# Row sums of |x - y| on one core: rows 5 and 6 in halves, the last row in five pieces instead of four

## The chip, the cores and the metric

One core of one Trainium2 chip. The time of a kernel is the device time in microseconds (us); "the time" of a set of runs is their median. Every run told of here is fast (granted clock 1.00, and none over 1.5% above the fastest of its kernel). Ratios are the mean time of one kernel's fast runs over that of the other's fast runs of the same rounds, so they are not quite the ratio of the medians quoted beside them.

## The reference

```python
batch, dim = 1024, 4096
x, y = two float32 arrays of (1024, 4096), normally distributed
np.sum(np.abs(x - y), axis=-1).astype(np.float32)      # 1024 sums
```

The inputs are 33.55 MB, the output 4 KB.

## The kernel before

Each of 128 partitions has eight rows, `K = 8`, of `C = 4096` columns. Rows 0 to 3 (`xa`, `yb`) come first; rows 4 to 7 of x go to `xb`, and rows 4 to 7 of y go into the places of `yb` that the first four subtractions free (`H = 4`). VectorE subtracts, ScalarE takes the absolute value and sums along the row as it goes. The last row, row 7, comes in pieces, so that little is left to do after the last byte.

```python
PIECES = [1984, 1088, 640, 384]
ROW6 = [2048, 1024, 1024]
# ... (helpers that place the instructions, tensors, semaphores: cut)
    put(lambda: nc.sync.dma_start(out=xb[:, 0:H - 1, :], in_=xr[:, H:K - 1, :]).then_inc(s_xb, 16))
    for k in range(H - 1):                      # y of rows 4, 5, 6
        put(lambda: nc.sync.wait_ge(s_sub, k + 1))
        put(lambda: nc.sync.dma_start(out=yb[:, k, :], in_=yr[:, H + k, :]).then_inc(s_row[k], 16))
    o = 0
    for i, w in enumerate(PIECES):              # row 7, x and y of each piece
        c = slice(o, o + w)
        put(lambda: nc.sync.dma_start(out=xb[:, H - 1, c], in_=xr[:, K - 1, c]).then_inc(s_piece[i], 16))
        if i == 0:
            put(lambda: nc.sync.wait_ge(s_sub, H))
        put(lambda: nc.sync.dma_start(out=yb[:, H - 1, c], in_=yr[:, K - 1, c]).then_inc(s_piece[i], 16))
        o += w
# ... sub() is a subtraction on VectorE, absum() the ScalarE instruction after it
    for k in range(H - 2):                      # rows 4 and 5 whole
        sub(xb[:, k, :], yb[:, k, :], ([(s_xb, 16)] if k == 0 else []) + [(s_row[k], 16)])
        absum(xb[:, k, :], ro[:, H + k:H + k + 1], s_act)
    o = 0
    for i, w in enumerate(ROW6):                # row 6 in three
        c = slice(o, o + w)
        sub(xb[:, H - 2, c], yb[:, H - 2, c], [(s_row[H - 2], 16)] if i == 0 else [])
        absum(xb[:, H - 2, c], part6[:, i:i + 1], s_act)
        o += w
    # ... row 7: each piece but the last is subtracted and summed like this, into last[:, i];
    # the last is only subtracted, into last[:, n_part:], and a reduction then takes
    # the absolute value of the whole of `last` and sums it:
            put(lambda: nc.vector.wait_ge(s_end, n_part + 2))
            put(lambda: nc.vector.reduce_sum(out=ro[:, K - 1:K], in_=last, axis=AX, apply_absolute_value=True).then_inc(s_end, 1))
```

Of the kernel before, what the change touches and what calls it, by code (L numbers as in the profile page):

```python
# [5 lines left out]

F32 = mybir.dt.float32
ABS = mybir.ActivationFunctionType.Abs
AX = mybir.AxisListType.X

F32 = mybir.dt.float32
ABS = mybir.ActivationFunctionType.Abs
AX = mybir.AxisListType.X

PIECES = [1984, 1088, 640, 384]
ROW6 = [2048, 1024, 1024]


class Entry:


    def __init__(self, nc):
        self.nc = nc

    def put(self, emit, before="UnconditionalBranch"):
        nc = self.nc
        hook = nc.inst_callbacks[-1]
        lower = nc._always_lower_symbolic_ap
        nc.remove_inst_callback(hook)
        nc._always_lower_symbolic_ap = False  # L30
        here = nc.cur_bb.bb.instructions
        n = len(here)
        try:
            emit()
        finally:
            nc._always_lower_symbolic_ap = lower
            nc.push_inst_callback(hook)
        here = nc.cur_bb.bb.instructions
        main = nc.main_func.blocks[0].instructions
        while len(here) > n:  # L40
            mine = here.pop(n)
            first = next(i for i, x in enumerate(main) if x.engine == mine.engine and x.opcode == before)
            main.insert(first, mine)

    def at_end(self, emit):

        nc = self.nc
        hook = nc.inst_callbacks[-1]
        here = nc.cur_bb.bb.name
        done = []  # L50

        def closing(ins):
            if done or nc.cur_bb.bb.name == here or ins.engine != mybir.EngineType.SP:
                return
            done.append(ins)
            emit()

        nc.remove_inst_callback(hook)
        nc.push_inst_callback(closing)
        nc.push_inst_callback(hook)  # L60


@with_exitstack
def kernel(ctx, tc, x, y, axis, out):
    nc = tc.nc
    P = nc.NUM_PARTITIONS
    R, C = x.shape
    K = R // P
    xr = x.rearrange("(p k) c -> p k c", p=P, k=K)
    yr = y.rearrange("(p k) c -> p k c", p=P, k=K)  # L70
    orr = out.rearrange("(p k) -> p k", p=P, k=K)
    assert sum(PIECES) == C and sum(ROW6) == C
    n_part = len(PIECES) - 1
    n6 = len(ROW6)
    H = K // 2
    entry = Entry(nc)
    put = entry.put

    def sbuf(name, shape):
        return nc.alloc_sbuf_tensor(name, shape, F32).ap()  # L80

    xa = sbuf("xa_rows", [P, H, C])
    xb = sbuf("xb_rows", [P, H, C])

    yb = sbuf("yb_rows", [P, H, C])
    ro = sbuf("ro_sums", [P, K])
    part6 = sbuf("part6_sums", [P, n6])

    last = sbuf("last_piece", [P, n_part + PIECES[-1]])

    s_first = tc.alloc_semaphore("s_first")
    s_xb = tc.alloc_semaphore("s_xb")
    s_row = [tc.alloc_semaphore(f"s_row{k}") for k in range(H - 1)]
    s_piece = [tc.alloc_semaphore(f"s_piece{i}") for i in range(len(PIECES))]
    s_sub = tc.alloc_semaphore("s_sub")
    s_act = tc.alloc_semaphore("s_act")
    s_end = tc.alloc_semaphore("s_end")
    s_out = tc.alloc_semaphore("s_out")


    put(lambda: nc.sync.dma_start(out=xa, in_=xr[:, 0:H, :]).then_inc(s_first, 16), before="RegisterMove")
    put(lambda: nc.scalar.dma_start(out=yb, in_=yr[:, 0:H, :]).then_inc(s_first, 16), before="RegisterMove")
    put(lambda: nc.sync.dma_start(out=xb[:, 0:H - 1, :], in_=xr[:, H:K - 1, :]).then_inc(s_xb, 16))
    for k in range(H - 1):
# [3 lines that stand above are left out]
    for i, w in enumerate(PIECES):  # L108
# [8 lines that stand above are left out]
    count = [0, 0]  # L117

    def sub(tx, ty, waits):
        for s, v in waits:  # L120
            put(lambda: nc.vector.wait_ge(s, v))
        put(lambda: nc.vector.tensor_sub(out=tx, in0=tx, in1=ty).then_inc(s_sub, 1))  # L122
        count[0] += 1

    def absum(tx, to, sem):
        put(lambda: nc.scalar.wait_ge(s_sub, count[0]))
        put(lambda: nc.scalar.activation(tx, tx, ABS, accum_out=to).then_inc(sem, 1))  # L127
        count[1] += sem is s_act

    for k in range(H):  # L130
        sub(xa[:, k, :], yb[:, k, :], [(s_first, 32)] if k == 0 else [])
        absum(xa[:, k, :], ro[:, k:k + 1], s_act)
    for k in range(H - 2):
        sub(xb[:, k, :], yb[:, k, :], ([(s_xb, 16)] if k == 0 else []) + [(s_row[k], 16)])
        absum(xb[:, k, :], ro[:, H + k:H + k + 1], s_act)
    o = 0
    for i, w in enumerate(ROW6):
        c = slice(o, o + w)
        sub(xb[:, H - 2, c], yb[:, H - 2, c], [(s_row[H - 2], 16)] if i == 0 else [])
        absum(xb[:, H - 2, c], part6[:, i:i + 1], s_act)  # L140
        o += w
    done6 = count[1]
    o = 0
    for i, w in enumerate(PIECES):
        c = slice(o, o + w)
        tx, ty = xb[:, H - 1, c], yb[:, H - 1, c]
        if i == 1:
            put(lambda: nc.vector.wait_ge(s_act, done6))
            put(lambda: nc.vector.reduce_sum(out=ro[:, K - 2:K - 1], in_=part6, axis=AX).then_inc(s_end, 1))  # L149
        if i < n_part:  # L150
            sub(tx, ty, [(s_piece[i], 32)])
            absum(tx, last[:, i:i + 1], s_end)
        else:
            put(lambda: nc.vector.wait_ge(s_piece[i], 32))
            put(lambda: nc.vector.tensor_sub(out=last[:, n_part:n_part + w], in0=tx, in1=ty).then_inc(s_end, 1))  # L155
# [4 lines that stand above are left out]
    put(lambda: nc.sync.wait_ge(s_end, n_part + 3))  # L160
    put(lambda: nc.sync.dma_start(out=orr, in_=ro).then_inc(s_out, 16))
    entry.at_end(lambda: nc.sync.wait_ge(s_out, 16))


# [1 line left out]
_INS = ['x', 'y', 'axis']  # L166
_OUTS = [((1024,), 'float32')]

_NUMBERS = {'axis': -1}


# [26 lines left out]
```

## Time and profile before

| | before |
|---|---|
| time, median of 6 runs | 85.92 us (85.87 to 85.97); three of them, 85.94, were known when the prediction was made |
| span of the profiled run | 84.1 us |
| VectorE busy, ScalarE busy | 36.5 us (43%), 31.2 us (37%) |
| read from memory over the span | 33.55 MB, 399 GB/s |
| row 6's y landed, last piece landed | 70.40, 80.59 us |
| last subtraction ended, ScalarE ended, closing reduction | 81.17, 81.33, 81.36 to 81.92 us |

A landing is read off the timeline: where an instruction is marked as released by a load ("<-DMA"), it starts 0.02 us after the landing. In all lines shown, DVE is VectorE, ACT is ScalarE, SPq and ACTq are the instruction queues of SyncE and ScalarE, and L122 is line 122 of the kernel. Neither compute engine is busy half of the span, and the loads run until 80 us. So only the order of events after the loads' end can be shortened, and the loads' end itself. The lines are in the prediction.

### The profile page before, as it was taken

To read this page: it belongs to the slowest core of one execution; us is meant where nothing else is said; L and a number is where in the kernel's file an instruction comes from. 1 tells how busy PE (TensorE), PEld (TensorE's weight loads), DVE (VectorE), ACT (ScalarE), POOL (GpSimd) and SP (SyncE) were. 2 spreads that over 40 slices of the span, in tenths; PEclk is the share of its full clock that TensorE was granted. 3 is DMA by queue.
4 is the path that set the end of the run, shared out by engine and by line. 5 is a ranking of instruction groups with operands and counts; after the bars stand their busy time and mean duration, and the time that the engine had idled before them with its cause. 6 is when DMAs were issued, how large, how long until landed. Compare 5 with 4: busy or idle time off the path is not lost.

```text
span 84.1 us, 97 instructions
## 1 busy us (share of the span) xinstructions
DVE 36.5 (43%) x15; ACT 31.2 (37%) x25; POOL 0.2 (0%) x4
## 2 busy tenths in 40 slices
DVE  0000000000000000000399999999199897988770
ACT  5000000000000000000002979797970977999960
POOL 0000000000000000000000000000000000000000
DMA  9289999992999999479899888899999999999900
GB/s 499 125 374 499 499 499 499 499 436 125 436 499 499 499 499 499 187 343 467 374 491 631 374 374 374 374 397 460 405 444 421 421 448 385 419 411 406 366 4 2
DMA packets 2160, 33.56 MB, mean 399 GB/s; under 512 B 368, under 2 KB 624, under 8 KB 1392
## 3 DMA queue, kind: packets, MB, share of 16 engines
q1 hardware_dynamic: 2016, 25.17, 71.2%
q10 hardware_dynamic: 144, 8.39, 23.0%
HBM read 33.55 MB, written 0.00 MB: 399 GB/s over the span
## 4 chain that ended last, share of the span: by engine, by line
DMA 67%; DVE 16%; ACT 13%; ACTq 1%; issue 0%
DMA yb_rows<-in_y_dram 67%; ACT xb_rows L127 13%; DVE xa_rows L122 10%; DVE xb_rows L122 5%; ACTq L193 1%; DVE ro_sums L157 1%
## 5 line engine op out<-in xcount | busy, mean ns | idle before, releaser
L122 DVE TENSOR_TENSOR xa_rows<-xa_rows,yb_rows 128x4096 f32<-128x4096 f32 x4 | 17.4, 4420 | 41.4 <-DMA yb_rows<-in_y_dram 41.4
L127 ACT ACTIVATE xa_rows<-xa_rows 128x4096 f32<-128x4096 f32 x4 | 14.5, 3617 | 45.5 <-DVE xa_rows L122 45.5
L122 DVE TENSOR_TENSOR xb_rows<-xb_rows,yb_rows 128x4096 f32<-128x4096 f32 (+5 forms) x8 | 17.8, 2240 | 3.5 <-DMA yb_rows<-in_y_dram 3.4
L127 ACT ACTIVATE xb_rows<-xb_rows 128x4096 f32<-128x4096 f32 (+5 forms) x8 | 14.9, 1858 | 3.7 <-DVE xb_rows L122 3.7
L127 ACT ACT_TABLE_LOAD x1 | 1.3, 1283 | 0.9 <-PEq L179 0.9
L127 ACT ACTIVATION_READ_ACCUMULATOR xb_rows<-xb_rows 128x1 f32 x8 | 1.5, 188 | 0.0
L127 ACT ACTIVATION_READ_ACCUMULATOR xa_rows<-xa_rows 128x1 f32 x4 | 0.7, 186 | 0.0
L157 DVE TENSOR_REDUCE ro_sums<-last_piece 128x1 f32<-128x387 f32 x1 | 0.6, 556 | 0.2 <-ACT xb_rows L127 0.2
L155 DVE TENSOR_TENSOR last_piece<-xb_rows,yb_rows 128x384 f32<-128x384 f32 x1 | 0.6, 558 | 0.2 <-DMA yb_rows<-in_y_dram 0.2
L149 DVE TENSOR_REDUCE ro_sums<-part_sums 128x1 f32<-128x3 f32 x1 | 0.2, 156 | 0.2 <-ACT xb_rows L127 0.2
L179 POOL MEMSET const-bfloat16-1.0<- 128x1 bf16 x1 | 0.1, 102 | 0.0
L179 POOL MEMSET const-uint8-127<- 128x1 uint8 x1 | 0.1, 102 | 0.0
L179 POOL MEMSET const-float32-0.0<- 128x1 f32 x1 | 0.1, 99 | 0.2 <-issue 0.2
L179 POOL MEMSET const-float32-1.0<- 128x1 f32 x1 | 0.1, 99 | 0.0
## 6 DMA issues: line engine op xcount, KB each, us to landing
xb_rows<-in_x_dram SPq DMA_DIRECT2D x1, 6144.0 KB, 54.8
yb_rows<-in_y_dram SPq DMA_DIRECT2D x3, 2048.0 KB, 15.3
xb_rows<-in_x_dram SPq DMA_DIRECT2D x1, 992.0 KB, 17.9
yb_rows<-in_y_dram SPq DMA_DIRECT2D x1, 992.0 KB, 16.4
xb_rows<-in_x_dram SPq DMA_DIRECT2D x1, 544.0 KB, 17.4
yb_rows<-in_y_dram SPq DMA_DIRECT2D x1, 544.0 KB, 18.2
xb_rows<-in_x_dram SPq DMA_DIRECT2D x1, 320.0 KB, 18.6
yb_rows<-in_y_dram SPq DMA_DIRECT2D x1, 320.0 KB, 18.9
```

What stands on the lines that cost most here:

```text
L122: put(lambda: nc.vector.tensor_sub(out=tx, in0=tx, in1=ty).then_inc(s_sub, 1))
L127: put(lambda: nc.scalar.activation(tx, tx, ABS, accum_out=to).then_inc(sem, 1))
L149: put(lambda: nc.vector.reduce_sum(out=ro[:, K - 2:K - 1], in_=part6, axis=AX).then_inc(s_end, 1))
L155: put(lambda: nc.vector.tensor_sub(out=last[:, n_part:n_part + w], in0=tx, in1=ty).then_inc(s_end, 1))
L157: put(lambda: nc.vector.reduce_sum(out=ro[:, K - 1:K], in_=last, axis=AX, apply_absolute_value=True).then_inc(s_end, 1))
L179: nc = _bacc.Bacc("TRN2", target_bir_lowering=False, num_devices=1)
L193: with _tile.TileContext(nc) as tc:
```

## The change

Row 5 was subtracted whole, so ScalarE could start on it only 4.5 us after it had landed; halves let ScalarE start sooner. Row 6 goes from three parts to two. A fifth piece in the last row makes the last one smaller (288 columns for 384), which shortens the last subtraction and the closing reduction, and the first one too (1728 for 1984), so that ScalarE can start on the last row sooner. The small reduction that joins the parts of rows 5 and 6 moves from before the second to before the third piece.

```diff
-PIECES = [1984, 1088, 640, 384]
-ROW6 = [2048, 1024, 1024]
+PIECES = [1728, 1056, 640, 384, 288]
+HALVES = [2048, 2048]
...
-    for k in range(H - 2):
-        sub(xb[:, k, :], yb[:, k, :], ([(s_xb, 16)] if k == 0 else []) + [(s_row[k], 16)])
-        absum(xb[:, k, :], ro[:, H + k:H + k + 1], s_act)
-    (row 6 in ROW6 parts, into part6)
+    sub(xb[:, 0, :], yb[:, 0, :], [(s_xb, 16), (s_row[0], 16)])
+    absum(xb[:, 0, :], ro[:, H:H + 1], s_act)
+    for k in (1, 2):
+        o = 0
+        for i, w in enumerate(HALVES):
+            c = slice(o, o + w)
+            sub(xb[:, k, c], yb[:, k, c], [(s_row[k], 16)] if i == 0 else [])
+            absum(xb[:, k, c], half[:, k - 1, i:i + 1], s_act)
+            o += w
...
-        if i == 1:
+        if i == 2:
-            put(lambda: nc.vector.reduce_sum(out=ro[:, K - 2:K - 1], in_=part6, axis=AX).then_inc(s_end, 1))
+            put(lambda: nc.vector.reduce_sum(out=ro[:, K - 3:K - 1], in_=half, axis=AX).then_inc(s_end, 1))
```

More of the change, by code (lines that the diff above doesn't have):

```diff
@@ L71 @@
     orr = out.rearrange("(p k) -> p k", p=P, k=K)
-    assert sum(PIECES) == C and sum(ROW6) == C
+    assert sum(PIECES) == C and sum(HALVES) == C
     n_part = len(PIECES) - 1
-    n6 = len(ROW6)
+    n2 = len(HALVES)
     H = K // 2
@@ L86 @@
     ro = sbuf("ro_sums", [P, K])
-    part6 = sbuf("part6_sums", [P, n6])
+    half = sbuf("half_sums", [P, 2, n2])
     last = sbuf("last_piece", [P, n_part + PIECES[-1]])
@@ L132 @@
         absum(xa[:, k, :], ro[:, k:k + 1], s_act)
-    for k in range(H - 2):
-        sub(xb[:, k, :], yb[:, k, :], ([(s_xb, 16)] if k == 0 else []) + [(s_row[k], 16)])
-        absum(xb[:, k, :], ro[:, H + k:H + k + 1], s_act)
-    o = 0
-    for i, w in enumerate(ROW6):
-        c = slice(o, o + w)
-        sub(xb[:, H - 2, c], yb[:, H - 2, c], [(s_row[H - 2], 16)] if i == 0 else [])
-        absum(xb[:, H - 2, c], part6[:, i:i + 1], s_act)
-        o += w
-    done6 = count[1]
+    sub(xb[:, 0, :], yb[:, 0, :], [(s_xb, 16), (s_row[0], 16)])
[7 more added lines that the diff above has]
+            o += w
+    done56 = count[1]
     o = 0
@@ L146 @@
         tx, ty = xb[:, H - 1, c], yb[:, H - 1, c]
-        if i == 1:
-            put(lambda: nc.vector.wait_ge(s_act, done6))
-            put(lambda: nc.vector.reduce_sum(out=ro[:, K - 2:K - 1], in_=part6, axis=AX).then_inc(s_end, 1))
+        if i == 2:
+            put(lambda: nc.vector.wait_ge(s_act, done56))
+            put(lambda: nc.vector.reduce_sum(out=ro[:, K - 3:K - 1], in_=half, axis=AX).then_inc(s_end, 1))
         if i < n_part:
```

## The prediction

> **What bounds the kernel now.** I read the chain that ended last first, in order of time; then the timeline of the last twelve microseconds; then the issues on the sync engine's queue; then the bytes moved in two stretches near the end.
>
> ```profile
> 41.38 8.77 DVE xa_rows L122 x2
> 50.15 0.02 issue
> 50.17 15.34 DMA yb_rows<-in_y_dram
> 65.51 0.02 issue
> 65.53 4.44 DVE xb_rows L122
> 69.97 0.02 issue
> 69.99 10.61 ACT xb_rows L127 x12
> ```
>
> The chain is loads up to 65.51 us. Then row 5 is subtracted whole (65.53 to 69.97) and from 69.99 the chain lies on ScalarE with no break. So ScalarE is formally the last bound. How close the next one is, the timeline tells:
>
> ```profile
> 70.42 4.56 DVE L122 TENSOR_TENSOR xb_rows<-xb_rows,yb_rows 128x2048 f32<-128x2048 f32 x3 [0.46 <-DMA yb_rows<-in_y_dram]
> 75.25 2.22 DVE L122 TENSOR_TENSOR xb_rows<-xb_rows,yb_rows 128x1984 f32<-128x1984 f32 x1 [0.26 <-DMA yb_rows<-in_y_dram]
> 77.58 1.84 ACT L127 ACTIVATE xb_rows<-xb_rows 128x1984 f32<-128x1984 f32 x1
> 77.70 0.16 DVE L149 TENSOR_REDUCE ro_sums<-part_sums 128x1 f32<-128x3 f32 x1 [0.23 <-ACT xb_rows L127]
> 79.42 1.09 ACT L127 ACTIVATE xb_rows<-xb_rows 128x1088 f32<-128x1088 f32 x1
> 79.62 0.82 DVE L122 TENSOR_TENSOR xb_rows<-xb_rows,yb_rows 128x640 f32<-128x640 f32 x1 [0.38 <-DMA yb_rows<-in_y_dram]
> 80.51 0.72 ACT L127 ACTIVATE xb_rows<-xb_rows 128x640 f32<-128x640 f32 x1
> 80.61 0.56 DVE L155 TENSOR_TENSOR last_piece<-xb_rows,yb_rows 128x384 f32<-128x384 f32 x1 [0.16 <-DMA yb_rows<-in_y_dram]
> 81.14 0.19 ACT L127 ACTIVATION_READ_ACCUMULATOR xb_rows<-xb_rows 128x1 f32 x1
> 81.36 0.56 DVE L157 TENSOR_REDUCE ro_sums<-last_piece 128x1 f32<-128x387 f32 x1 [0.19 <-ACT xb_rows L127]
> ```
>
> What to see: the subtraction of the last piece started at 80.61, released by a load, and ended at 80.61 + 0.56 = 81.17. ScalarE's last accumulator read ended at 81.14 + 0.19 = 81.33. The closing reduction waited for both, so ScalarE ended it by only 81.33 - 81.17 = **0.16 us**. The load path lies right behind, and it is nearly the whole kernel: 33.55 MB read at a mean of 399 GB/s. No arrangement of the engines' work takes more than some tenths from the end. Also: each "<-DMA" start gives a landing time (start less 0.02): row 6 at 70.40, the 1984 piece at 75.23, the 640 piece at 79.60, the 384 piece at 80.59.
>
> ```profile
> 61.15 0.43 SPq L110 DMA_DIRECT2D xb_rows<-in_x_dram  x1
> 61.63 2.70 SPq L113 DMA_DIRECT2D yb_rows<-in_y_dram  x1
> ```
>
> The last of eight piece loads took 2.70 us to issue where the others took about 0.45. [...]It comes back as a rival.
>
> ```profile
> 65.50:70.40 4.90, 4.43 (x1) 3.78 (x3) 0.00 (x0) 1.00 1.00 425
> 75.23:79.60 4.37, 3.67 (x3) 4.37 (x9) 0.00 (x0) 1.00 1.02 395
> ```
>
> The last column is GB/s. With a whole row in flight it is 425, with pieces 395, at a DMA share of 1.0 in both: pieces move fewer bytes per microsecond, so a fifth piece isn't free.
>
> [...]
>
> **The change, part by part.**
>
> *Loads.* Eight piece loads become ten; the earlier rows' loads and their waits stay. What a pair of piece loads (x and y) costs beyond its bytes I estimate from the landings. Row 5 landed at 65.51 and row 6 at 70.40: 2.097 MB in 4.89 us, 429 GB/s; row 4 to row 5 gives about 435. I take 432. The four pieces, 4.194 MB, took 80.59 - 70.40 = 10.19 us where 432 GB/s would give 9.71. So 0.48 us for four pairs, **0.12 us a pair**. Check on the first pair alone: 2.032 MB in 4.83 us against 4.70, 0.13 us. So new landings, each bytes/432 + 0.12 after the one before: 1728 columns (1.769 MB) 70.40 + 4.22 = 74.62; 1056: + 2.62 = 77.24; 640: + 1.64 = 78.88; 384: + 1.03 = 79.91; 288: + 0.80 = **80.71**. The last byte's landing moves out by 0.12 us.
>
> *VectorE.* Row 5 in halves of 2292 ns, overlapping by some 0.08 us (the three row 6 instructions of before sum to 4.73 and fill 4.56): 65.53 to about 70.03, still before row 6 lands. Row 6: 70.42 to 74.92, as before. [...]Starts follow the landing or the engine, whichever is later: 1728 at 74.9 to 76.86 (the engine, not the load, releases it); 1056 at 77.26 to 78.52; the small reduction at 78.54 to 78.70, in the gap before the 640 piece, where it no longer waits for ScalarE (which is done with row 6 by 76.9); 640 at 78.90 to 79.72; 384 at 79.93 to 80.49; 288 at 80.73 to **81.19**.
>
> *ScalarE.* Before, row 5 began at 69.99, when the whole row was subtracted. Now its first half is ready at 67.82, but ScalarE is on row 4 until 65.17 + 3.62 = 68.79. So: half at 68.79 to 70.68, half to 72.57, one microsecond sooner than before (73.61). Row 6 halves: 72.73 (ready then) to 74.62, and 74.94 to 76.83. Pieces[...]: 1728 at 76.88 to 78.51, 1056 at 78.54 to 79.61, 640 at 79.74 to 80.46, 384 at 80.51 to 81.02, its accumulator read ending near **81.11**. ScalarE has gaps again; one more instruction (13 in place of 12) and its 0.19 us are beside the loads.
>
> *The end.* Both paths arrive within 0.1 us: 81.19 (load, subtraction) and 81.11. The reduction over 292 columns in place of 387 is 95 columns shorter, 95 x 1.042 = 0.10 us: 0.46. It runs from 81.22 to 81.68; before it ended at 81.92. The output's transfer and the close are unchanged. Sum: first start of the reduction 0.14 earlier (0.16 of ScalarE's lateness gone, 0.10 off the last subtraction, less 0.12 for the landing), and 0.10 off the reduction: **0.24 us**. 85.94 - 0.24 = **85.70 us**.
>
> **The rivals.** (1) The extra pair costs nothing on the loads. Then the landing stays 80.59, ScalarE's end at about 81.08 decides, and the reduction ends at 81.57: 85.59. For it: one pair's cost lies near the trace's own jitter (row loads differ by 0.07 us). Against: four pairs together show 0.48. (2) Packets of 288 columns (1152 bytes) cost more than larger ones, say twice my 0.12: the landing is 80.83, the end 81.80, the time 85.82; at three times the gain is nearly gone. For it: 395 GB/s late against 412 for the first piece's stretch. Against: the 384 piece came 0.99 us after the 640 piece, and 0.91 + 0.12 = 1.03 would have been allowed. (3) [...]I estimate the last issue ends near 72 us, eight before its data's turn, so no harm; if it stalled past 79 us, the time would be above 86. (4) ScalarE is the bound and the whole microsecond by which it is ahead after row 5 is gained: 84.9. For it: the chain of waits names ScalarE for 12.7% of the span. Against: the load-released subtraction ends at 81.17 already, so at most 0.16 of it counts.
>
> **Range and chances.** Rival 1 gives 85.59 and rival 2 85.82; the three times of before spread 0.08 us and a different trace may shift the landing by 0.1. So 85.45 to 85.92 for 8 in 10. Two per cent is 1.72 us, seven times what any step here offers, and a slowing of that size needs rival 3 in full: faster 0.01, within 2% 0.98, slower 0.01.
>
> **What would show it.** Right: ScalarE's row 5 starts near 68.8 and it waits for VectorE several times after 72; the small reduction has no ScalarE wait; the subtraction of 288 columns starts near 80.73 after a load, takes 458 ns, and the closing reduction takes about 460 and follows that subtraction (the chain ends on loads, not on twelve ScalarE instructions). Wrong: a landing of the last piece at 80.6 or below (rival 1) or above 80.8 (rival 2); a sync issue that ends after 79 (rival 3); rows 5 or 6 landing at other times than 65.5 and 70.4, which nothing here foresees; or the 1056-column ScalarE instruction still running at 79.9.

Rival 3 is that the last loads are issued too late; its 72 us stands as the author's estimate. The sum came to 0.24 us (0.16 + 0.10 - 0.12 + 0.10), the time to 85.70 us; the start and end times, and with them the 0.10 off the last subtraction, used durations. The trace of before gives about the same ones, as estimates. A straight line through its subtractions of 2048 and 384 columns (2292 and 558 ns, so 1.042 ns a column) has 1958 ns at 1728 columns, 1258 at 1056 and 458 at 288, 100 less than at 384. A line through its ScalarE instructions of 2048 and 640 columns (1894 and 722 ns, 0.832 ns a column) has 1628, 1068 and, at 384 columns, 509 ns. The 1.042 ns a column of the closing reduction is in that trace too: 556 ns for 387 columns and 156 for 3. So is the order on ScalarE: from 70 us on an accumulator read begins 0.09 to 0.10 us before its instruction ends (75.41 and 75.50), and the next instruction starts at that end.

## The result, and the profile after

| | before | after |
|---|---|---|
| time, median of 6 runs | 85.92 us (85.87 to 85.97) | 85.48 us (85.37 to 85.85) |
| ratio, 95% interval | | 0.9955 (0.9935 to 0.9974) |
| span of the profiled run | 84.1 us | 83.7 us |
| row 6's y landed, last piece landed | 70.40, 80.59 | 70.39, 80.43 |
| last subtraction ended, ScalarE ended | 81.17, 81.33 | 80.91, 80.96 |
| closing reduction | 81.36 to 81.92 | 80.99 to 81.45 |

The time fell by 0.44 us, half a per cent. The end of the chain that ended last, in order of time (start us, us, what):

```profile
54.51 15.88 DMA yb_rows<-in_y_dram
70.39 0.02 issue
70.41 4.51 DVE xb_rows L122 x2
74.92 0.02 issue
74.94 5.51 ACT xb_rows L127 x8
80.45 0.41 ACTq L194
80.86 0.10 ACT xb_rows L127
80.97 0.02 issue
80.99 0.46 DVE ro_sums L158
```

Row 5 has left the chain: loads reach to row 6 at 70.39, and ScalarE's unbroken stretch is 5.5 us from 74.94, where it was 10.6 us from 69.99. The timeline, where it answers to the lines of before (start us, us, engine, line, operation, and in brackets the idle time before it and its releaser):

```profile
68.77 1.89 ACT L127 ACTIVATE xb_rows<-xb_rows 128x2048 f32<-128x2048 f32 x1
74.94 1.91 ACT L127 ACTIVATE xb_rows<-xb_rows 128x2048 f32<-128x2048 f32 x1 [0.20 <-DVE xb_rows L122]
76.85 1.63 ACT L127 ACTIVATE xb_rows<-xb_rows 128x1728 f32<-128x1728 f32 x1
77.20 1.26 DVE L122 TENSOR_TENSOR xb_rows<-xb_rows,yb_rows 128x1056 f32<-128x1056 f32 x1 [0.42 <-DMA yb_rows<-in_y_dram]
78.38 0.15 DVE L150 TENSOR_REDUCE ro_sums<-half_sums 128x2 f32<-128x4 f32 x1
78.76 1.49 DVE L122 TENSOR_TENSOR xb_rows<-xb_rows,yb_rows 128x640 f32<-128x640 f32 x2 [0.24 <-DMA yb_rows<-in_y_dram]
80.45 0.46 DVE L156 TENSOR_TENSOR last_piece<-xb_rows,yb_rows 128x288 f32<-128x288 f32 x1 [0.20 <-DMA yb_rows<-in_y_dram]
80.77 0.19 ACT L127 ACTIVATION_READ_ACCUMULATOR xb_rows<-xb_rows 128x1 f32 x1
80.99 0.46 DVE L158 TENSOR_REDUCE ro_sums<-last_piece 128x1 f32<-128x292 f32 x1
```

The first half of row 5 starts on ScalarE at 68.77, and ScalarE waits for VectorE again at 74.94. The last subtraction starts at 80.45, after a load: the last piece landed at 80.43, **earlier** than the 80.59 of before, though there is one pair of loads more. The prediction had that the other way round (80.71), and most of the experiments are about it. Both paths still meet at the end, within 0.05 us; ScalarE is the later one.

The sync engine's queue after the change:

```profile
61.64 2.67 SPq L113 DMA_DIRECT2D yb_rows<-in_y_dram  x1
64.35 3.51 SPq L110 DMA_DIRECT2D xb_rows<-in_x_dram  x1
67.91 1.75 SPq L113 DMA_DIRECT2D yb_rows<-in_y_dram  x1
```

The first seven piece loads took 0.33 to 0.46 us each to issue, the last three 2.67, 3.51 and 1.75; the last ended at 69.66, more than ten microseconds before its data landed at 80.43. So the end does not wait for these long issues; what makes them long is not shown. And the stretch of pieces (the stretch, its length, the busy us of VectorE, ScalarE and POOL, the TensorE clock, the DMA share, GB/s):

```profile
75.23:79.60 4.37, 3.70 (x4) 4.37 (x6) 0.00 (x0) 1.00 1.04 403
```

403 GB/s where the kernel before had 395.

### The profile page after: what moved, and what is told of

Read it like the earlier page. It is cut to its first block, busy times and chain, and to the rows that moved or that the text cites. A ratio compares the mean times of both kernels' runs of the same rounds, so it can differ in the third digit from the quotient of the medians.

```text
span 83.7 us, 102 instructions
## 1 busy us (share of the span) xinstructions
DVE 36.3 (43%) x16; ACT 31.6 (38%) x27; POOL 0.2 (0%) x4
## 4 chain that ended last, share of the span: by engine, by line
DMA 68%; DVE 22%; ACT 7%; ACTq 0%; issue 0%
DMA yb_rows<-in_y_dram 68%; DVE xa_rows L122 16%; ACT xb_rows L127 7%; DVE xb_rows L122 5%; DVE ro_sums L158 1%; ACTq L194 0%
## 5 line engine op out<-in xcount | busy, mean ns | idle before, releaser
L122 DVE TENSOR_TENSOR xb_rows<-xb_rows,yb_rows 128x2048 f32<-128x2048 f32 (+5 forms) x9 | 17.9, 2020 | 3.4 <-DMA yb_rows<-in_y_dram 3.3
L127 ACT ACTIVATE xb_rows<-xb_rows 128x2048 f32<-128x2048 f32 (+5 forms) x9 | 15.2, 1686 | 2.9 <-DVE xb_rows L122 2.8
L156 DVE TENSOR_TENSOR last_piece<-xb_rows,yb_rows 128x288 f32<-128x288 f32 x1 | 0.5, 459 | 0.2 <-DMA yb_rows<-in_y_dram 0.2
L158 DVE TENSOR_REDUCE ro_sums<-last_piece 128x1 f32<-128x292 f32 x1 | 0.5, 457 | 0.1
```

The source lines that it names most:

```text
L122: put(lambda: nc.vector.tensor_sub(out=tx, in0=tx, in1=ty).then_inc(s_sub, 1))
L127: put(lambda: nc.scalar.activation(tx, tx, ABS, accum_out=to).then_inc(sem, 1))
L156: put(lambda: nc.vector.tensor_sub(out=last[:, n_part:n_part + w], in0=tx, in1=ty).then_inc(s_end, 1))
```

## The experiments

Two questions. First, which part of the change gains: the halves, the smaller last piece, or only both together? My theory was that the two paths at the end are tied, so that neither part alone gains; the rivals were each part by itself. Second, why did the last piece land earlier?

The table has one row per kernel. Those from e1 on were timed in five rounds, in three groups of four (e1 to e4, e5 to e8, e9 to e12), each group on one chip in the same rounds as the kernel before. "640 piece" is the time from the start of the second piece's subtraction to that of the third, both released by landings, where the third has 640 columns. "Row 6 to last" is the time from the start of row 6's first subtraction to that of the last piece's; both start when their load has landed, so it is the time that the last row's loads took. All three columns on the right come from the profiled run of each kernel.

| kernel | time (us) | ratio to before (95%) | 640 piece | row 6 to last | closing reduction ended |
|---|---|---|---|---|---|
| before | 85.92 | 1 | 1.66 | 10.19 | 81.92 |
| after | 85.48 | 0.9955 (0.9935 to 0.9974) | 1.56 | 10.04 | 81.45 |
| e1 after again | 85.45 | 0.9946 (0.9934 to 0.9958) | 1.56 | 10.06 | 81.53 |
| e2 halves only | 85.97 | 0.9999 (0.9987 to 1.0011) | 1.66 | 10.27 | 81.98 |
| e3 pieces only | 86.14 | 1.0018 (1.0006 to 1.0030) | - | 10.15 | 82.08 |
| e4 four loads | 85.86 | 0.9991 (0.9979 to 1.0004) | 1.55 | 10.35 | 81.78 |
| e5 aligned | 85.89 | 0.9995 (0.9978 to 1.0011) | 1.65 | 10.30 | 81.86 |
| e6 shifted | 85.78 | 0.9980 (0.9966 to 0.9994) | 1.55 | 9.90 | 81.74 |
| e7 reduce early | 85.57 | 0.9958 (0.9944 to 0.9971) | 1.56 | 10.05 | 81.54 |
| e8 row 5 whole | 86.05 | 1.0007 (0.9994 to 1.0021) | 1.60 | 10.14 | 82.06 |
| e9 SBUF shift | 85.71 | 0.9967 (0.9954 to 0.9981) | 1.61 | 9.99 | 81.62 |
| e10 memory shift | 85.61 | 0.9959 (0.9944 to 0.9973) | 1.60 | 10.01 | 81.55 |
| e11 all half-way | 85.53 | 0.9945 (0.9930 to 0.9960) | 1.56 | 9.94 | 81.31 |
| e12 six pieces | 85.36 | 0.9945 (0.9912 to 0.9979) | - | 10.04 | 81.41 |

(The dash of e3: its third subtraction was not released by the load; e12 has no 640 piece, and its row 6 comes in two loads, so its 10.04 is counted from the landing of the second. The kernel before ran at 85.92, 85.96 and 85.97 in the three groups. All results were correct.)

### e1: the changed kernel once more

No edit.

> The changed kernel once more, for a second trace of it. Theory (both paths meet at the end): last piece's subtraction released near 80.45, closing reduction at 81.0, time 0.44 +- 0.1 us below before. If the earlier landing of the last piece (80.43 where 80.71 was forecast) was one execution's luck, this trace has it at 80.6 to 80.7 and the time is about 85.7.

It came out at 85.45, and the last subtraction started at 80.57 with row 6 landing 0.10 later than in the first trace. Counted from row 6, the loads took 10.06 us, as in the first trace (10.04). So the earlier landing is no luck of one execution. It also tells how to read landings: the absolute times shift by about 0.1 us from run to run. The differences from row 6 are steadier, but not to 0.02 us: kernels with these same loads of the last row have 10.04 (after), 10.06 (e1), 10.05 (e7), 10.15 (e3) and 10.14 (e8), and before and e2, whose loads are again the same, 10.19 and 10.27. With one trace each, a difference under 0.1 us says nothing.

### e2: only the halves

```diff
-PIECES = [1728, 1056, 640, 384, 288]
+PIECES = [1984, 1088, 640, 384]
```

> Rows 5 and 6 in halves, the last row in the old four pieces (small reduction after the second piece). Theory: ScalarE is still held at the end by the 640 piece (subtracted by 80.44, then 0.72 + 0.10) and ends near 81.28, so halves alone gain about 0.05 us: 85.87. Rival (the halves are what gained): the time falls by 0.3 or more, to 85.6 or below.

Ratio 0.9999: the halves alone gain nothing. The timeline shows why (kernel e2):

```profile
77.62 1.86 ACT L127 ACTIVATE xb_rows<-xb_rows 128x1984 f32<-128x1984 f32 x1 [0.66 <-DVE xb_rows L122]
79.69 0.82 DVE L122 TENSOR_TENSOR xb_rows<-xb_rows,yb_rows 128x640 f32<-128x640 f32 x1 [0.31 <-DMA yb_rows<-in_y_dram]
80.57 0.72 ACT L127 ACTIVATE xb_rows<-xb_rows 128x640 f32<-128x640 f32 x1
81.42 0.56 DVE L158 TENSOR_REDUCE ro_sums<-last_piece 128x1 f32<-128x387 f32 x1 [0.16 <-ACT xb_rows L127]
```

The 640 piece landed at 79.67, its subtraction ended at 80.51, and ScalarE, which had to finish the 1088 piece first, was done with it at 81.39 (80.57 + 0.72, and 0.10 for the rest of the accumulator read). ScalarE's backlog of row 5 is gone: it even waited 0.66 us for the first piece. It ends as late as before because that piece still has 1984 columns. It is subtracted only at 77.60, and from 77.62 ScalarE works through the three pieces without a gap, 3.77 us. In the changed kernel the first piece has 1728 columns and ScalarE starts on it at 76.85. (This is read from the traces; no run varies the first piece alone.) The last subtraction of e2 ended at 81.26 (80.70 + 0.56), so the load path would have left little to gain either.

### e3: only the pieces

The kernel before with

```diff
-PIECES = [1984, 1088, 640, 384]
+PIECES = [1728, 1056, 640, 384, 288]
```

> Rows 5 and 6 as before, the last row in the new five pieces. Theory: ScalarE starts the first piece at 77.58 as before, and with one more instruction ends at about 81.6; the reduction of 292 columns ends near 82.1, so the time rises by about 0.15 us: 86.08. Rival (the smaller last piece is what gained): the time falls by 0.3 or more, to 85.6 or below.

It became slower by 0.2 us, ratio 1.0018, as the theory had it. From the chain of kernel e3:

```profile
69.99 11.00 ACT xb_rows L127 x13
80.99 0.09 ACTq L193
81.08 0.51 ACT xb_rows L127 x2
81.59 0.02 issue
81.62 0.46 DVE ro_sums L157
```

ScalarE has no gap from 69.99 to 81.59. The last subtraction was done at 81.05 (80.59 + 0.46); the smaller piece was ready and had to wait for ScalarE's backlog, to which the fifth piece added one instruction. So neither part gains alone, and the two together do.

### e8: row 5 whole, everything else changed

```diff
-    for k in (1, 2):
+    sub(xb[:, 1, :], yb[:, 1, :], [(s_row[1], 16)])
+    absum(xb[:, 1, :], ro[:, H + 1:H + 2], s_act)
+    for k in (2,):
...
-            ... reduce_sum(out=ro[:, K - 3:K - 1], in_=half, ...
+            ... reduce_sum(out=ro[:, K - 2:K - 1], in_=half[:, 1, :], ...
```

> The changed kernel with row 5 whole again; row 6 stays in halves, the last row in five pieces. Theory: row 5's split is what frees ScalarE; without it ScalarE starts row 5 at 69.99, the first piece at about 77.4 and ends near 81.42, and the time is 85.93. Rival (row 6's halves carry it): about 85.5.

86.05 us, ratio 1.0007, against 0.9958 for e7 in the same rounds: the gain is gone. ScalarE ended at 81.57. Of the two rows it is row 5's split that frees ScalarE; row 6's halves do not carry it without row 5's. (The reverse, row 5 in halves with row 6 left in three parts, was not run.)

### e7: the small reduction in its old place

```diff
-        if i == 2:
+        if i == 1:
```

> The changed kernel with the small reduction back ahead of the second piece, where the kernel before had it. Theory: ScalarE is done with row 6 at about 76.95, the reduction runs 76.98 to 77.13, before the second piece lands at 77.18, so nothing changes: 85.48. Rival (the place of the reduction is part of the gain): the second piece's subtraction starts late by 0.1 or more and the time rises by 0.1 or more.

Ratio 0.9958, the changed kernel's own 0.9955. In its trace the reduction ran from 77.08 to 77.24 and the second piece's subtraction started at 77.30; in e1, where row 6's subtraction started 0.01 us sooner, it started at 77.29. Moving the reduction is no part of the gain.

### e4: three more pairs of loads

The prediction's term for the loads was 0.12 us for each pair. This kernel adds three pairs and leaves the arithmetic as it is:

```diff
+LOADS = [4, 1, 1, 1, 1]
...
-        c = slice(o, o + w)
-        (one load of x and one of y)
+        n = LOADS[i]
+        for j in range(n):
+            c = slice(o + j * (w // n), o + (j + 1) * (w // n))
+            (one load of x and one of y, on the same semaphore)
...
-            sub(tx, ty, [(s_piece[i], 32)])
+            sub(tx, ty, [(s_piece[i], 32 * LOADS[i])])
```

> The changed kernel with the first piece of 1728 columns loaded as four pairs of 432, with no change to the arithmetic: three more pairs of loads. If a pair costs 0.12 us as the prediction had it, the last piece lands 0.36 us later and the time is 0.36 us above the changed kernel's, 85.84. If pairs are free, it stays at 85.48. [...]

85.86 us, 0.41 above e1 in the same rounds. From the timeline of kernel e4:

```profile
77.54 1.26 DVE L125 TENSOR_TENSOR xb_rows<-xb_rows,yb_rows 128x1056 f32<-128x1056 f32 x1 [0.61 <-DMA yb_rows<-in_y_dram]
80.77 0.46 DVE L159 TENSOR_TENSOR last_piece<-xb_rows,yb_rows 128x288 f32<-128x288 f32 x1 [0.16 <-DMA yb_rows<-in_y_dram]
```

Row 6 to last took 10.35 us in place of 10.04 to 10.06: 0.3 us for three pairs, **0.10 us a pair**, near the predicted 0.12. The last issue of this kernel ended at 71.66, nine microseconds before its piece landed at 80.75, so a late issue is not the reason. The size is rough. The added loads start at columns 432, 864 and 1296, none a multiple of 64, and in the next experiments three moved starts go with 0.15 to 0.37 us; and other kernels that differ by one pair give 0.04 us (e11 against e6) and 0.03 to 0.11 (e5 against e2 and before), each within the scatter. So the added pairs did cost, and yet the kernel with five pieces is done loading 0.15 us before the one with four. Something else about the new pieces must be worth the 0.15 and the cost of the pair together, about a quarter of a microsecond.

### e5 and e6: where the pieces start

The old pieces start at columns 1984, 3072 and 3712, all multiples of 64 (256 bytes). The new ones start at 1728, 2784, 3424 and 3808, of which the last three lie half-way between two multiples. (Starts are counted from the start of the row; no view shows addresses.) The 640 piece itself, the same size in both, takes 1.66 us with the old and 1.56 with the new (1.60 in e8). e5 keeps five pieces, all at multiples of 64; e6 has four with three of the starts half-way:

```diff
-PIECES = [1728, 1056, 640, 384, 288]
+PIECES = [1728, 1088, 640, 384, 256]        # e5
+PIECES = [1952, 1088, 640, 416]             # e6
```

> The changed kernel with pieces of 1728, 1088, 640, 384 and 256 columns: still five, but now every piece starts at a multiple of 64 columns (256 bytes), as all four did in the kernel before; in the changed kernel the last three start half-way between such multiples. The 640 piece came 1.66 us after its predecessor in both kernels with the old pieces and 1.55 us in all three with the new. If the start column is what makes old pieces slower, the 640 piece takes 1.66 here again, the last lands near 80.7 and the time is about 85.65. If it is the number or the order of the loads, the 640 piece takes 1.55, the last lands near 80.4 and the time is 85.4 to 85.5.

> Rows in halves with four pieces of 1952, 1088, 640 and 416: as the halves alone, but the last three pieces start half-way between multiples of 64 columns. If the start column matters, the 640 piece comes 1.55 us after its predecessor, the last lands near 80.45 and the time is about 85.75 (the last piece and its reduction are longer). If it is the number of loads, the 640 piece takes 1.66, the last lands near 80.65 and the time is about 85.95.

In both, the 640 piece took the time that the expectation gave for the start column. From the timelines, e5 first:

```profile
77.50 1.29 DVE L122 TENSOR_TENSOR xb_rows<-xb_rows,yb_rows 128x1088 f32<-128x1088 f32 x1 [0.58 <-DMA yb_rows<-in_y_dram]
79.15 0.82 DVE L122 TENSOR_TENSOR xb_rows<-xb_rows,yb_rows 128x640 f32<-128x640 f32 x1 [0.30 <-DMA yb_rows<-in_y_dram]
80.85 0.42 DVE L156 TENSOR_TENSOR last_piece<-xb_rows,yb_rows 128x256 f32<-128x256 f32 x1
81.44 0.42 DVE L158 TENSOR_REDUCE ro_sums<-last_piece 128x1 f32<-128x260 f32 x1 [0.17 <-ACT xb_rows L127]
```

then e6:

```profile
77.77 1.29 DVE L122 TENSOR_TENSOR xb_rows<-xb_rows,yb_rows 128x1088 f32<-128x1088 f32 x1 [0.41 <-DMA yb_rows<-in_y_dram]
79.32 0.83 DVE L122 TENSOR_TENSOR xb_rows<-xb_rows,yb_rows 128x640 f32<-128x640 f32 x1 [0.19 <-DMA yb_rows<-in_y_dram]
```

The 640 piece took 1.65 us with five pieces at multiples of 64, and 1.55 with four at half-way starts: it goes with the start, not with the number of pieces. Row 6 to last was 10.30 in e5 against 10.04 to 10.06 in the changed kernel, and 9.90 in e6 against 10.27 in e2: three starts moved by 32 columns are worth about 0.25 us in the one and 0.37 in the other. With the scatter told under e1 that is 0.15 to 0.26 us for five pieces (e5 against after, e1, e3, e7 and e8) and 0.29 to 0.37 for four (e6 against before and e2).

The kept traces also hold how long each DMA packet took, though no view prints it. The 640 piece is 256 packets of 2560 bytes. In the ten kernels that have it with half-way starts (e9 and e10, below, on one side only) at least 252 of them took 102 ns; in before and e5 only 112 did, and others up to 115 ns. But in e2, at multiples of 64 as well, 255 did, and only its 384 piece had many slower packets (55 of 256). So from the 640 piece on, slower packets in number were seen only with starts at multiples of 64, and even there not for every piece. A second part comes after the data: from the end of the last piece's last data packet to its landing it took 0.44 to 0.45 us in before, e2 and e5, and 0.29 to 0.36 in all eleven others. What lies behind either is not shown.

In time e5 missed my number: 85.89 where I had expected 85.65. The step that I had left out there is ScalarE: its 384 piece landed 0.5 us later than in the changed kernel, was subtracted by 80.76, and ScalarE ended at 81.42, 0.15 after the last subtraction. So **with its pieces at multiples of 64 columns the change gains nothing that these runs show** (0.9995, interval 0.9978 to 1.0011). e6 was as expected, 85.78 for 85.75.

### e9 and e10: in the input's memory or in SBUF?

Both move the last three pieces by 32 columns in SBUF against their place in the row; e9 has starts at multiples of 64 in the inputs, e10 half-way ones.

```diff
-PIECES = [1728, 1056, 640, 384, 288]
+PIECES = [1984, 1088, 640, 384]             # e9
+PIECES = [1952, 1088, 640, 416]             # e10
+SHIFT = 32
...
-    xb = sbuf("xb_rows", [P, H, C])
+    xb_all = sbuf("xb_rows", [P, H * C + SHIFT])
+    xb = xb_all[:, 0:H * C].rearrange("p (h c) -> p h c", h=H, c=C)
     (yb likewise; the pieces of row 7 lie at o for the first and o + SHIFT for the others)
```

> The halves alone with pieces of 1984, 1088, 640 and 384, which start at multiples of 64 columns in the inputs; in SBUF the last three lie 32 columns further on, so there they start half-way. If the start in the input's memory is what counts, the 640 piece takes 1.66 us after its predecessor, row 6 to the last landing takes 10.2 us, and the time is 85.95. If the start in SBUF counts, 1.55 us, 9.9 us and about 85.7.

> The reverse: pieces of 1952, 1088, 640 and 416, which start half-way in the inputs, laid 32 columns further on in SBUF, so there they start at multiples of 64. If the start in the input's memory counts, the 640 piece takes 1.55 us, row 6 to last landing 9.9 us, and the time is 85.78, as with the shifted four pieces. If the start in SBUF counts, 1.66, 10.25 and 85.95 to 86.1.

Neither expectation came true as written. Both kernels lie between: the 640 piece took 1.61 and 1.60 us, row 6 to last 9.99 and 10.01. That does not set them apart from the half-way kernels, since e8 has 1.60 too. In their packets they are like those: all 256 packets of the 640 piece took 102 ns, and the last piece landed 0.30 and 0.34 us after its data. What e9 does show is that the starts in the input's memory cannot be all of it, since they are those of e2 and before, and its loads took 0.28 and 0.20 us less. More I don't claim, for the two have a flaw: `xb_rows` is longer by 128 bytes in them, which may have moved `yb_rows`, allocated after it, by as much. I have not verified that, but row 6 landed at 70.17 and 70.20 in these two and at 70.34 to 70.56 in the other whole-row kernels, before any piece was loaded; so something moved for all loads of y, and x and y pieces may have had different starts. Which side counts, and whether it matters that both are shifted alike, stays open.

### e11 and e12: using it

e11 moves the one start of the changed kernel that is a multiple of 64. e12 goes further: six pieces, all starts half-way, and row 6's y in two loads.

```diff
-PIECES = [1728, 1056, 640, 384, 288]
+PIECES = [1760, 1024, 640, 384, 288]              # e11
+PIECES = [1632, 1024, 576, 384, 256, 224]         # e12
+SPLIT6 = [2080, 2016]                             # e12: y of row 6 in two loads, a semaphore each
```

> The changed kernel with pieces of 1760, 1024, 640, 384 and 288: all four inner starts half-way, where the changed kernel has one of four at a multiple of 64. If each such start saves about 0.11 us, row 6 to the last landing takes 9.94 in place of 10.05; ScalarE and VectorE keep up almost, and the time falls by 0.05 to 0.1, to about 85.4. If the effect is spent, 85.48.

> An attempt to beat both: six pieces of 1632, 1024, 576, 384, 256 and 224 with all starts half-way, and row 6's y in two loads of 2080 and 2016 columns, so that VectorE is done with row 6 before the pieces come. From the landings so far (about 2.39 ns a column and 0.04 us a pair at a half-way start) the last piece lands near 80.45, its reduction ends near 81.3, and the time is about 85.3. If two further loads in the queue cost 0.12 us each, it is 85.5 or above.

e11's loads took 9.94 us, the 9.94 expected, and its traced end is 0.14 us before the changed kernel's (the traced run, 85.34, was the fastest of its six). Its time, 85.53, ratio 0.9945, is not to be told from the changed kernel's (0.9955 and 0.9946). e12 has the lowest median of all, 85.36, and five of its six runs lie from 85.26 to 85.43, but one took 86.22, and its interval (0.9912 to 0.9979) covers those of the others. Its last reduction ended at 81.41 in the trace, where 81.3 was expected, with the last landing at 80.57 for the expected 80.45. Neither is shown to beat the changed kernel.

## Why the prediction was right, point by point

The time, 85.48, lies in the range, close to its lower edge; the traced gain is 0.47 us where the sum had 0.24. That it still fell inside the range is partly luck: the lower edge had been drawn for a free pair and for jitter, not for what the start of a piece does. Two of the prediction's own signs came out wrong: the last piece landed below 80.6, which was to mean a free pair, and the chain ended on ScalarE, by 0.05 us, and not on a load.

- **ScalarE's half of row 5**: forecast to start at 68.79, started at 68.77. First piece on ScalarE: 76.88, measured 76.85. Durations of VectorE's and ScalarE's new shapes were within 20 ns of the lines through before's own durations (288 columns 458 and 459, 1728 columns 1958 and 1952, 1056 on ScalarE 1068 and 1083).
- **No ScalarE wait for the small reduction**: true, and e7 shows that it is worth nothing.
- **The reduction over 292 columns**: 0.46 forecast, 457 ns measured, 0.10 off the end.
- **At most a few tenths, because the load path lies 0.16 us behind ScalarE**: true, and rival 4 (84.9 us) is out. ScalarE did gain the forecast microsecond after row 5, and the time fell by 0.44. e2 and e3 sharpen it: ScalarE's backlog and the sizes of the pieces have to change together.
- **Late issues** (rival 3): the long issue is there, and became three (2.70 us before; 2.67, 3.51 and 1.75 after); the last one ended at 69.66, sooner than the estimate of 72. Its data landed at 80.43, so nothing waited for it.
- **The term that was mis-sized**: "The last byte's landing moves out by 0.12 us." It moved in by 0.16, a difference of 0.28 us. (Counted from row 6, the five traces with these loads have 10.04 to 10.15 us where the sum has 10.31; e3, at 10.15, is hardly below the 10.19 of before.) Of that 0.23 reached the end, since ScalarE became the last by 0.05. The reason is not rival 1 (a free pair): e4 measured about 0.10 us a pair. The 0.12 and the 432 GB/s had been fitted to pieces that all start at multiples of 64 columns, and applied to pieces of which three don't. e5 is the test: with all starts at multiples of 64 the five pieces took 10.30 us after row 6, and the prediction's own sum is 80.71 - 70.40 = 10.31. The fit held for pieces like those it came from; that the start is a variable of its own, worth 0.15 to 0.37 us for three starts, was not in it. e5 also shows how little is left without it: ratio 0.9995, though there the second piece is 32 columns larger as well, which delays the third and fourth by some 0.08 us.

Shown: that both parts are needed; that three more pairs of loads moved the landing out by 0.3 us; that with half-way starts the last row landed sooner, by 0.15 to 0.37 us in traces that scatter by 0.1. Not shown: the mechanism behind the start column, on which side of the transfer it acts, and what one pair costs to better than some hundredths.

## What to carry to other kernels

When two paths end within some tenths of each other (here 0.16 us), a change to one of them alone can gain nothing (e2, ratio 0.9999), and a change that shortens one and lengthens the other can lose (e3, 1.0018); try the parts apart before you drop or keep them. Split a load's tail by where the pieces start as well as by their size: here three starts moved 32 columns to the side were worth 0.15 to 0.37 us, about as much as three pairs of loads (0.3 us in e4). A cost fitted from a trace holds for the shapes and places that the trace had (here the fit gave 10.31 us from row 6 to last: e5, with starts like those of the fit, took 10.30, the changed kernel 10.04), so ask of each new piece in what else it differs.
